# Score products of two heads, or of two maps, recorded alternately and issued as one set

## Chip, cores and metric

The kernel runs on one core of a Trainium2 chip. The metric is device microseconds of one execution, from the first to the last instruction and what lies around them; smaller is better. Engines are named as in the profile: PE is TensorE's matmul, PEld its weight load, DVE VectorE, ACT ScalarE, POOL GpSimd, SP the engine that issues the DMAs.

## What is computed

The reference runs two transformer blocks of two layers each on 256 tokens of width 1024, in fp32. A layer of block 1 is a gated feed-forward layer, a mixer and a second feed-forward layer; a layer of block 2 is a mixer and a feed-forward layer. The mixer of block 1 has four kinds of attention with four heads each, whose outputs are joined and projected:

- na: each token sees a window of a 4 x 64 grid, with a bias that is learned; head width 64
- diff: two maps per head, each from query and key of width 32, `a = softmax(s1) - lam * softmax(s2)`, with `s = q k^T / sqrt(32)`
- gqa: four query heads, two key and value heads, width 64, plain softmax
- dil: a mixture of three dilated windows, width 64

```python
        s = jnp.einsum('ibhqd,ibhkd->ibhqk', qblk, k12).astype(jnp.float32) * scale
        p = jax.nn.softmax(s, axis=-1)
        a = p[0] - lam * p[1]
        return jnp.einsum('bhqk,bhkd->bhqd', a.astype(vt.dtype), vt)
```

The mixer of block 2 has fox (4 causal heads with a decay), moba (4 causal heads of width 64 with a relative bias) and mla (8 causal heads of width 96). In both blocks a head is: scores q k^T, softmax, product with v.

## The kernel before, in words

**A plan, then the issue.** Nothing is issued while the kernel's functions run. Each call records an instruction in `Plan.add` (line 100), with what it depends on, the tiles that it touches and a cost in ns (`cost`, line 148; a matmul of rounded fp32, F32R, costs n / 2.4 + 2.5 ns for n columns). `order` (line 179) then places all instructions of the program by a list schedule with priorities from a backward pass (`priorities` and `backward`, lines 306 and 324), and `issue` (line 301) emits them in that order, so each engine's stream is fixed before the chip runs. All are emitted at one line, so all rows of the profile say L304, and groups are told by their tiles. Matmuls of one head can so be parted by any other PE work.

**Precision.** Operands are split into a high and a low F32R part. `mm3` (line 607) makes a product of three matmuls, high x high, high x low, low x high, added up in PSUM. moba, fox and mla use plain fp32 instead, with one matmul each.

**Mixers.** `mixer1` (line 1041) and `mixer2` (line 1398) run the input projection in chunks of 512 columns (`inproj`, line 986), prepare q and k (norm, rotation, transposes to the tiles qkT) and start attention heads as soon as their inputs are recorded. A head is a generator: `diff_job` (line 928), `job` (line 885, for dil, gqa and na) or `causal_job` (line 1339, for mla, fox and moba). `pump` (line 728) takes every started generator one step further after each half chunk and starts one more job of a list, with at most six in flight. `outproj` (line 1012) follows, and the last heads run beside it.

**One head.** `job` takes one PSUM bank (`aps`, line 749, tile att), writes the scores of 2 x 128 queries against 256 keys into it (two `mm3`, six matmuls of 256 columns), and has DVE and ACT make the softmax. Then come four transposes (tile tp, `turn_p`, line 919), a copy to SBUF (tile pt), the product with v into another bank (att<-V,pt), and a division. `diff_job` makes two maps so, i = 0 and i = 1, twelve matmuls of 256 columns in two banks. `causal_job` makes two matmuls, of 128 and of 256 columns.

**Rows of the array.** A matmul uses the rows of the array that correspond to the partitions of its operands. For head h, `mixer1` takes partitions 64 * (h % 2) on of dil and na, 64 * (h // 2) on of gqa; moba takes 64 * (h % 2) on. These products use 64 rows, of the upper or of the lower half. diff uses 32 rows, those from here on:

```python
            b = 64 * (h % 2) + 32 * i
            for t in range(2):
                tok = slice(t * P, t * P + P)
                self.mm3(sc[:, t * S:t * S + S], qT[0][b:b + 32, tok], qT[1][b:b + 32, tok], kT[0][b:b + 32], kT[1][b:b + 32], True, True)
```

mla and fox use 96 and 66 rows. In the profile's rows, 64*128 and 32*128 ahead of the shape are the rows and columns of the array. PSUM banks for att come from the four banks of tag y during the input projection, and in turn from tags mm and y during the output projection.

Of the kernel before, what the change touches and what calls it, by code (L numbers as in the profile page):

```python
# [72 lines left out]
class Plan:  # L73
# [26 lines left out]
    def add(self, eng, method, args, kw):  # L100
# [42 lines left out]
        self.ops.append([eng, method, args, kw, sorted(deps), sorted(touch), cost, after, table])  # L143

# [307 lines left out]
class Net:  # L452
# [432 lines left out]
    def job(self, kind, l, h, q, k, vh, col, bias=None):  # L885

        nc, V = self.nc, self.nc.vector
        sc = self.aps()
        for t in range(2):
            self.mm3(sc[:, t * S:t * S + S], q[0][:, t * P:t * P + P], q[1][:, t * P:t * P + P], *k, True, True)  # L890
        p = self.m(512, "p")
        nm = self.sm.tile([P, 2], F32, tag="nm", name="nm")
        if bias is not None:
            e = self.m(512, "e")
            for t in range(2):
                V.tensor_tensor_reduce(e[:, t * S:t * S + S], sc[:, t * S:t * S + S], bias[:, t], -0.125, 3e38,
                                       ALU.add, ALU.min, nm[:, t:t + 1])
            for t in range(2):
                nc.scalar.activation(p[:, t * S:t * S + S], e[:, t * S:t * S + S], AF.Exp, bias=nm[:, t:t + 1], scale=-1.0)
        else:  # L900
            V.tensor_reduce(nm, sc.rearrange("p (t k) -> p t k", t=2), axis=AX.X, op=ALU.max, negate=True)
            V.tensor_scalar(nm, nm, 0.125, None, op0=ALU.mult)
            for t in range(2):
                nc.scalar.activation(p[:, t * S:t * S + S], sc[:, t * S:t * S + S], AF.Exp, bias=nm[:, t:t + 1], scale=0.125)
        yield
        pt = self.turn_p(p)
        yield
        pv = self.aps()
        for t in range(2):
            for kt in range(2):  # L910
                nc.tensor.matmul(pv[:, t * 65:t * 65 + 65], lhsT=pt[:, (t * 2 + kt) * P:(t * 2 + kt + 1) * P],
                                 rhs=self.V[:, kt, vh, :], start=kt == 0, stop=kt == 1)
# [4 lines left out]
        self.done[kind] = self.done.get(kind, 0) + 1  # L917
# [10 lines left out]
    def diff_job(self, kind, l, h, qT, kT, vh, col):  # L928
# [3 lines left out]
        for i in range(2):  # L932
            sc = self.aps()
            b = 64 * (h % 2) + 32 * i
            for t in range(2):
# [105 lines left out]
    def mixer1(self, l, ydone, mid, pre):  # L1041
# [43 lines left out]
        for kind, vf, v0, col in (("dil", "v1", 4, 768), ("gqa", "vgqa", 8, 512), ("na", "vna", 10, 0)):  # L1085
            if kind == "na":
                self.jobs.append((lambda: True, lz(lambda: self.na_bias_mask(bias))))
            for h in range(4):
                def mk(kind=kind, v0=v0, col=col, h=h):
                    T = qkT[kind]  # L1090
                    b, base = (h % 2, 64 * (h // 2)) if kind == "gqa" else (h // 2, 64 * (h % 2))
                    kb = 0 if kind == "gqa" else h // 2
                    vh = v0 + (h // 2 if kind == "gqa" else h)
                    bb = None if kind == "gqa" else self.lnm if kind == "dil" else bias[h]
                    return self.job(kind, l, h, [a[base:base + 64, b] for a in T[0]], [a[base:base + 64, kb] for a in T[1]], vh, col + 64 * h, bb)
# [572 lines left out]
```

## Time and profile before

| what | us |
|---|---|
| median of three runs (lowest, highest) | 1653.28 (1652.83, 1656.73) |
| the profiled execution | 1654.43 |
| its span, first to last instruction | 1652.7 |
| PE busy | 1627.0 |
| DVE busy | 1085.4 |
| ACT busy | 842.3 |
| POOL busy | 167.9 |

The profiled execution lies 1.7 us above its span and 1.15 above the median. Mean granted clock of TensorE is 0.989 of full speed. The timeline gives the start and duration of instructions, and merges neighbours of one engine that have the same tiles into one row with their number (xN); its duration goes from the first start to the last end. As matmuls are pipelined, a row overlaps the next one: what PE spends on it is the distance to the next row's start.

### The profile page before, as it was taken

How to read it: one execution, taken by the hardware profiler on the slowest of the kernel's cores; microseconds unless marked ns; L12 is line 12 of the kernel's file. 1: busy time of each engine (PE TensorE's matmuls, PEld its weight loads, DVE VectorE, ACT ScalarE, POOL GpSimd, SP SyncE). 2: the span in 40 equal slices, each digit the busy share in tenths (PEclk: the TensorE clock that was granted, in tenths of full speed). 3: DMA queues.
4: the chain of work that ended last, by engine and by line, in shares of the span. 5: the costliest groups of instructions: out<-in, count | busy, mean ns of one | idle time of the engine just before them, and what ended most of it. 6: DMA issues, size and time to landing. Idle time of an engine off the chain costs nothing.

```text
span 1652.7 us, 21333 instructions
## 1 busy us (share of the span) xinstructions
PE 1627.0 (98%) x7912; PEld 1347.2 (82%) x7912; DVE 1085.4 (66%) x1956; ACT 842.3 (51%) x1384; POOL 167.9 (10%) x205
## 2 busy tenths in 40 slices
PE   9989999999999999999999999999999999999998
PEld 7868877888888888877788888888888888888886
DVE  6557778577777877777757645656755476585553
ACT  6544456554434444455554444576644358664442
POOL 0000056000000000035400000120000012000000
PEclk9989999999999999998899999999999999999999
DMA  8687762257776777763328645451645445245451
GB/s 305 221 268 283 264 220 103 77 224 301 267 293 245 300 293 267 289 220 120 110 75 311 245 178 195 171 180 53 242 180 202 153 162 207 101 171 202 176 203 51
DMA packets 81884, 335.78 MB, mean 203 GB/s; under 512 B 17136, under 2 KB 19700, under 8 KB 50676
## 3 DMA queue, kind: packets, MB, share of 16 engines
q1 hardware_dynamic: 81780, 334.42, 55.7%
q8 instruction: 62, 1.02, 0.2%
q14 instruction: 42, 0.34, 0.1%
HBM read 333.29 MB, written 2.84 MB: 203 GB/s over the span
## 4 chain that ended last, share of the span: by engine, by line
PE 92%; DVE 3%; POOL 2%; DMA 1%; issue 1%; ACT 1%; SPq 0%; POOLq 0%; DVEq 0%; ACTq 0%
PE mm L304 54%; PE y L304 27%; PE att L304 6%; PE tp L304 6%; DMA raw<-in_gu 1%; DVE wlo L304 1%; POOL rs L304 1%; POOL qk L304 0%; POOL rot L304 0%; DVE o L304 0%; DVE qk L304 0%; DVE ms L304 0%; DVE xl L304 0%; SPq L304 0%; DMA t5t<-in_t_table 0%
## 5 line engine op out<-in xcount | busy, mean ns | idle before, releaser
L304 DVE TENSOR_TENSOR wlo<-raw,whi 128x1024 fp32r<-128x1024 f32 (+2 forms) x516 | 607.2, 1211 | 263.2 <-ACT whi L304 261.4
L304 ACT CAST whi<-raw 128x1024 fp32r<-128x1024 f32 (+2 forms) x516 | 513.4, 1038 | 316.3 <-PE mm L304 132.1
L304 PE MATMUL mm<-whi,xh 128*128 128x512 f32 (+2 forms) x1376 | 547.0, 398 | 2.5 <-ACT whi L304 1.5
L304 PE MATMUL mm<-wlo,xh 128*128 128x512 f32 (+2 forms) x1376 | 537.3, 391 | 0.7 <-DVE wlo L304 0.7
L304 PE MATMUL mm<-whi,xl 128*128 128x512 f32 (+2 forms) x1376 | 534.8, 390 | 1.6 <-DVE xl L304 1.6
L304 PEld LDWEIGHTS mm<-whi,xl 128*128 128x128 f32 x1376 | 259.9, 189 | 55.7 <-DVE xl L304 2.9
L304 PEld LDWEIGHTS mm<-whi,xh 128*128 128x128 f32 x1376 | 259.9, 189 | 55.3 <-ACT whi L304 2.3
L304 PEld LDWEIGHTS mm<-wlo,xh 128*128 128x128 f32 x1376 | 260.4, 189 | 50.5 <-DVE wlo L304 1.6
L304 PE MATMUL y<-whi,hth 128*128 128x512 f32 x528 | 206.9, 393 | 0.0
L304 PE MATMUL y<-wlo,hth 128*128 128x512 f32 x528 | 206.6, 391 | 0.0
L304 PE MATMUL y<-whi,htl 128*128 128x512 f32 x528 | 206.5, 391 | 0.0
L304 POOL TENSOR_TENSOR rs<-rs,mhalf 128x1 f32<-128x1 f32 x28 | 27.2, 972 | 1267.2 <-DVE rs L304 1267.2
L304 ACT ACTIVATE sil<-mm 128x256 f32<-128x256 f32 x110 | 42.2, 384 | 210.4 <-PE mm L304 209.7
L304 DVE CUSTOM_DVE_ANT_0 ada<-ada,act 128x512 f32<-128x512 f32 x192 | 128.5, 688 | 17.3 <-DMA ada<-in_ada 16.9
L304 PEld LDWEIGHTS y<-wlo,hth 128*128 128x128 f32 x528 | 99.7, 189 | 21.6 <-issue 1.3
L304 PEld LDWEIGHTS y<-whi,htl 128*128 128x128 f32 x528 | 99.7, 189 | 20.9
L304 PEld LDWEIGHTS y<-whi,hth 128*128 128x128 f32 x528 | 99.5, 189 | 20.7 <-ACT whi L304 0.2
L304 DVE TENSOR_TENSOR hch<-mm,sil 128x256 f32<-128x256 f32 x110 | 46.3, 421 | 78.9 <-ACT sil L304 78.5
L304 PE MATMUL att<-qkT 64*128 64x256 f32 (+6 forms) x368 | 65.6, 321 | 1.8 <-DVE qkT L304 1.5
L304 POOL TENSOR_TENSOR rs<-ms,mhalf 128x2 f32<-128x2 f32 (+3 forms) x34 | 50.9, 1499 | 135.8 <-DVE ms L304 134.2
L304 PEld LDWEIGHTS att<-V,pt 128*128 128x128 f32 x448 | 59.5, 196 | 6.3 <-ACT pt L304 2.3
L304 PE MATMUL att<-V,pt 128*128 128x65 f32 (+1 forms) x448 | 60.0, 273 | 1.9 <-ACT pt L304 1.9
(158 smaller groups left out, 1388.1 us busy)
## 6 DMA issues: line engine op xcount, KB each, us to landing
raw<-in_gu SPq DMA_DIRECT2D x127, 1024.0 KB, 4.9
raw<-in_dn SPq DMA_DIRECT2D x66, 1024.0 KB, 4.9
ada<-in_ada SPq DMA_DIRECT2D x192, 256.0 KB, 5.3
raw<-in_in SPq DMA_DIRECT2D x32, 1024.0 KB, 4.8
raw<-in_out SPq DMA_DIRECT2D x16, 1024.0 KB, 4.8
row<-moddram SPq DMA_DIRECT2D x12, 512.0 KB, 6.8
raw<-in_in2a SPq DMA_DIRECT2D x4, 840.0 KB, 4.2
raw<-in_gu SPq DMA_DIRECT2D x6, 512.0 KB, 6.1
```

Of the source, the lines that this page charges most:

```text
L304: getattr(getattr(self.nc, eng), method)(*args, **kw)
```

## The change

Three things are done. In `diff_job` the matmuls of the two maps are recorded alternately (i = 0, i = 1, i = 0, ...), which makes six pairs with 32 rows each. `job` and `causal_job` take a list of heads and record the matmuls of two heads alternately: heads 0 and 1 and heads 2 and 3 of dil, na and moba, heads 0 and 2 and heads 1 and 3 of gqa, so that the two lie in different halves of the partitions. Each of the two has its own PSUM bank. And a new method `fuse` replaces the recorded matmuls by one entry of the plan, with the sum of their costs, all their dependencies and tiles; `issue` emits its matmuls one after the other. mla and fox keep one head a job, but their two matmuls become such an entry too. The rest of a head (softmax, transposes, product with v) is recorded per head as before, for both heads of a job within one step of the generator; there are half as many jobs of dil, gqa, na and moba.

```diff
@@ -141,6 +141,23 @@
+    def fuse(self, i0):
+        run = self.ops[i0:]
+        del self.ops[i0:]
+        eng = run[0][0]
+        assert all(o[0] == eng for o in run)
+        deps = sorted({d for o in run for d in o[4] if d < i0})
+        touch = sorted({t for o in run for t in o[5]})
+        self.ops.append([eng, "fused", [o[1:4] for o in run], {}, deps, touch, sum(o[6] for o in run), 0, None])
+        for a in self.write.values():
+            a[a > i0] = i0
+        for k, r in self.read.items():
+            if r and r[-1][0] > i0:
+                self.read[k] = [(min(j, i0), idx) for j, idx in r]
+        self.last_mm = i0
...
@@ -301,7 +318,8 @@
     def issue(self):
         for i in self.order(self.priorities())[0]:
             eng, method, args, kw = self.ops[i][:4]
-            getattr(getattr(self.nc, eng), method)(*args, **kw)
+            for m, a, k in args if method == "fused" else [(method, args, kw)]:
+                getattr(getattr(self.nc, eng), m)(*a, **k)
...
-    def job(self, kind, l, h, q, k, vh, col, bias=None):
+    def job(self, kind, heads):
...
-        sc = self.aps()
+        sc = [self.aps() for _ in heads]
+        i0 = len(nc.ops)
         for t in range(2):
-            self.mm3(sc[:, t * S:t * S + S], q[0][:, t * P:t * P + P], q[1][:, t * P:t * P + P], *k, True, True)
-        p = self.m(512, "p")
-        nm = self.sm.tile([P, 2], F32, tag="nm", name="nm")
-        if bias is not None:
-            e = self.m(512, "e")
+            for a, b, start, stop in ((0, 0, True, False), (0, 1, False, False), (1, 0, False, True)):
+                for s, (q, k, _, _, _) in zip(sc, heads):
+                    nc.tensor.matmul(s[:, t * S:t * S + S], lhsT=q[a][:, t * P:t * P + P], rhs=k[b], start=start, stop=stop)
+        nc.fuse(i0)
+        ps = []
+        for s, (_, _, _, _, bias) in zip(sc, heads):
+            p = self.m(512, "p")
...
+            ps.append(p)
+        yield
+        pts = [self.turn_p(p) for p in ps]
+        yield
+        for pt, (_, _, vh, col, _) in zip(pts, heads):
+            pv = self.aps()
...
+            self.weigh(pv, col)
+        self.done[kind] = self.done.get(kind, 0) + 2
...
+    def weigh(self, pv, col):
...
@@ -930,13 +961,17 @@
         for i in range(2):
-            sc = self.aps()
-            b = 64 * (h % 2) + 32 * i
-            for t in range(2):
-                tok = slice(t * P, t * P + P)
-                self.mm3(sc[:, t * S:t * S + S], qT[0][b:b + 32, tok], qT[1][b:b + 32, tok], kT[0][b:b + 32], kT[1][b:b + 32], True, True)
-            ps.append(sc)
-            V.tensor_reduce(nm[:, 2 * i:2 * i + 2], sc.rearrange("p (t k) -> p t k", t=2), axis=AX.X, op=ALU.max, negate=True)
+            ps.append(self.aps())
+        i0 = len(nc.ops)
+        for t in range(2):
+            tok = slice(t * P, t * P + P)
+            for a, c, start, stop in ((0, 0, True, False), (0, 1, False, False), (1, 0, False, True)):
+                for i in range(2):
+                    b = 64 * (h % 2) + 32 * i
+                    nc.tensor.matmul(ps[i][:, t * S:t * S + S], lhsT=qT[a][b:b + 32, tok], rhs=kT[c][b:b + 32], start=start, stop=stop)
+        nc.fuse(i0)
+        for i in range(2):
+            V.tensor_reduce(nm[:, 2 * i:2 * i + 2], ps[i].rearrange("p (t k) -> p t k", t=2), axis=AX.X, op=ALU.max, negate=True)
...
@@ -1085,14 +1120,17 @@
-            for h in range(4):
-                def mk(kind=kind, v0=v0, col=col, h=h):
+            for hs in ((0, 2), (1, 3)) if kind == "gqa" else ((0, 1), (2, 3)):
+                def mk(kind=kind, v0=v0, col=col, hs=hs):
...
+                    heads = []
+                    for h in hs:
+                        b, base = (h % 2, 64 * (h // 2)) if kind == "gqa" else (h // 2, 64 * (h % 2))
+                        kb = 0 if kind == "gqa" else h // 2
+                        vh = v0 + (h // 2 if kind == "gqa" else h)
+                        bb = None if kind == "gqa" else self.lnm if kind == "dil" else bias[h]
+                        heads.append(([a[base:base + 64, b] for a in T[0]], [a[base:base + 64, kb] for a in T[1]], vh, col + 64 * h, bb))
+                    return self.job(kind, heads)
                 self.jobs.append((has(kind, vf), lz(mk)))
...
-    def causal_job(self, kind, q, k, vh, col, bias, scale):
+    def causal_job(self, kind, heads, bias, scale):
...
-        sc = self.aps()
+        sc = [self.aps() for _ in heads]
         span = (slice(0, P), slice(P, 384))
+        i0 = len(nc.ops)
-            nc.tensor.matmul(sc[:, span[t]], lhsT=q[:, t * P:t * P + P], rhs=k[:, 0:P * (t + 1)], start=True, stop=True)
...
+            for s, (q, k, _, _) in zip(sc, heads):
+                nc.tensor.matmul(s[:, span[t]], lhsT=q[:, t * P:t * P + P], rhs=k[:, 0:P * (t + 1)], start=True, stop=True)
+        nc.fuse(i0)
+        ps = []
+        for i, s in enumerate(sc):
...
+            ps.append(p)
+        yield
+        pts = []
+        for p in ps:
...
+            pts.append(pt)
+        yield
+        for pt, (_, _, vh, col) in zip(pts, heads):
+            pv = self.aps()
...
+            self.weigh(pv, col)
+        self.done[kind] = self.done.get(kind, 0) + len(heads)
...
@@ -1432,21 +1478,24 @@
         def heads(kind, v0, g):
-            for h in range(4):
-                def mk(h=h):
...
+            for hs in [(h,) for h in range(4)] if kind == "fox" else [(0, 1), (2, 3)]:
+                def mk(hs=hs):
+                    A, bias = [], []
+                    for h in hs:
...
+                        A.append((q, k, v0 + h, g * 256 + 64 * h))
+                    return self.causal_job(kind, A, bias, 0.125)
                 J.append((has(kind, "v"), lz(mk)))
...
-                return self.causal_job("mla", st["q"][h // 2][0:96, h % 2], st["k"][h // 2][0:96, h % 2], 8 + h, 512 + 64 * h,
-                                       (self.causal[:, P:S], self.causal), 96 ** -0.5)
+                return self.causal_job("mla", [(st["q"][h // 2][0:96, h % 2], st["k"][h // 2][0:96, h % 2], 8 + h, 512 + 64 * h)],
+                                       [(self.causal[:, P:S], self.causal)], 96 ** -0.5)
```

## Rows read from the trace of the kernel before

**Rows 1.** The page: PE's share of the span, and the chain by engine.

```profile
PE 1627.0 (98%) x7912; PEld 1347.2 (82%) x7912; DVE 1085.4 (66%) x1956; ACT 842.3 (51%) x1384; POOL 167.9 (10%) x205
...
PE 92%; DVE 3%; POOL 2%; DMA 1%; issue 1%; ACT 1%; SPq 0%; POOLq 0%; DVEq 0%; ACTq 0%
```

**Rows 2.** Busy time in four stretches: start:end, length, engines, PEclk, DMA share, GB/s.

```profile
245.00:280.00 35.00, 34.19 (x195) 27.10 (x193) 34.38 (x90) 23.90 (x62) 22.77 (x27) 1.00 0.27 91
293.00:323.00 30.00, 30.00 (x206) 25.73 (x206) 16.44 (x47) 16.15 (x33) 3.06 (x3) 1.00 0.29 103
760.00:797.00 37.00, 36.03 (x188) 28.24 (x187) 31.30 (x81) 23.16 (x61) 24.97 (x26) 0.91 0.24 86
...
1128.00:1138.00 10.00, 10.00 (x74) 7.99 (x71) 7.45 (x32) 9.12 (x23) 0.19 (x1) 1.00 0.17 72
```

**Rows 3.** PE by line and form: count, busy us, mean ns, idle us before.

```profile
L304 PE MATMUL att<-qkT 64*128 64x256 f32 x160 | 30.0, 319 | 1.5 <-DVE qkT L304 1.5
...
L304 PE MATMUL att<-qkT 32*128 32x256 f32 x96 | 12.9, 318 | 0.3 <-ACT pd L304 0.3
...
L304 PE MATMUL att<-qkT 64*128 64x128 f32 x16 | 3.0, 320 | 0.0
```

**Rows 4.** PE timeline around a run of six: start us, duration us, instruction.

```profile
760.57 0.39 PE L304 MATMUL mm<-whi,xl 128*128 128x512 f32 x1
760.79 0.39 PE L304 MATMUL mm<-whi,xh 128*128 128x512 f32 x1
761.11 0.97 PE L304 MATMUL att<-qkT 32*128 32x256 f32 x6
762.01 0.49 PE L304 MATMUL mm<-wlo,xh 128*128 128x512 f32 x1
762.43 0.97 PE L304 MATMUL att<-qkT 32*128 32x256 f32 x6
```

**Rows 5.** PE timeline: one product, two in different rows, two serial, a mixed run.

```profile
312.19 0.38 PE L304 MATMUL att<-qkT 64*128 64x256 f32 x1
...
312.87 0.38 PE L304 MATMUL att<-qkT 64*128 64x256 f32 x2
...
321.76 0.50 PE L304 MATMUL att<-qkT 64*128 64x256 f32 x2
...
755.45 1.66 PE L304 MATMUL att<-qkT 32*128 32x256 f32 x24
```

**Rows 6.** PE timeline: first and last runs of gqa/na, dil, diff; three of moba.

```profile
242.76 0.58 PE L304 MATMUL att<-qkT 32*128 32x256 f32 x4
...
271.68 0.38 PE L304 MATMUL att<-qkT 64*128 64x256 f32 x1
...
293.52 0.97 PE L304 MATMUL att<-qkT 64*128 64x256 f32 x6
...
767.60 0.58 PE L304 MATMUL att<-qkT 32*128 32x256 f32 x1
...
803.32 1.43 PE L304 MATMUL att<-qkT 64*128 64x256 f32 x5
...
843.38 0.97 PE L304 MATMUL att<-qkT 64*128 64x256 f32 x6
...
1130.65 0.49 PE L304 MATMUL att<-qkT 64*128 64x128 f32 x2
...
1133.06 0.70 PE L304 MATMUL att<-qkT 64*128 64x256 f32 x2
...
1136.10 1.03 PE L304 MATMUL att<-qkT 64*128 64x128 f32 x8
...
1433.40 0.93 PE L304 MATMUL att<-qkT 64*128 64x128 f32 x8
```

**Rows 7.** A PE wait in its timeline, and the stretch behind it by windows.

```profile
799.87 1.97 PE L304 MATMUL att<-V,pt 128*128 128x65 f32 x8 [1.85 <-ACT pt L304]
...
799.70:810.00 10.30, 10.13 (x32) 7.85 (x33) 3.54 (x14) 3.58 (x8) 3.05 (x3) 0.50 0.13 56
```

More of the change, by code (lines that the diff above doesn't have):

```diff
@@ new lines, in job @@
+            for a, b, start, stop in ((0, 0, True, False), (0, 1, False, False), (1, 0, False, True)):
[5 more added lines that the diff above has]
+            p = self.m(512, "p")
+            nm = self.sm.tile([P, 2], F32, tag="nm", name="nm")
+            if bias is not None:
+                e = self.m(512, "e")
+                for t in range(2):
+                    V.tensor_tensor_reduce(e[:, t * S:t * S + S], s[:, t * S:t * S + S], bias[:, t], -0.125, 3e38,
+                                           ALU.add, ALU.min, nm[:, t:t + 1])
+                for t in range(2):
+                    nc.scalar.activation(p[:, t * S:t * S + S], e[:, t * S:t * S + S], AF.Exp, bias=nm[:, t:t + 1], scale=-1.0)
+            else:
+                V.tensor_reduce(nm, s.rearrange("p (t k) -> p t k", t=2), axis=AX.X, op=ALU.max, negate=True)
+                V.tensor_scalar(nm, nm, 0.125, None, op0=ALU.mult)
+                for t in range(2):
+                    nc.scalar.activation(p[:, t * S:t * S + S], s[:, t * S:t * S + S], AF.Exp, bias=nm[:, t:t + 1], scale=0.125)
+            ps.append(p)
@@ new lines, in job @@
+        yield
[3 more added lines that the diff above has]
+            pv = self.aps()
+            for t in range(2):
+                for kt in range(2):
+                    nc.tensor.matmul(pv[:, t * 65:t * 65 + 65], lhsT=pt[:, (t * 2 + kt) * P:(t * 2 + kt + 1) * P],
+                                     rhs=self.V[:, kt, vh, :], start=kt == 0, stop=kt == 1)
+            self.weigh(pv, col)
+        self.done[kind] = self.done.get(kind, 0) + 2
@@ new lines, in causal_job @@
+            for s, (q, k, _, _) in zip(sc, heads):
[3 more added lines that the diff above has]
+        for i, s in enumerate(sc):
+            p = self.m(384, "p")
+            e = self.m(384, "e")
+            nm = self.sm.tile([P, 2], F32, tag="nm", name="nm")
+            for t in range(2):
+                V.tensor_tensor_reduce(e[:, span[t]], s[:, span[t]], bias[i][t], -scale, 3e38, ALU.add, ALU.min, nm[:, t:t + 1])
+            for t in range(2):
+                nc.scalar.activation(p[:, span[t]], e[:, span[t]], AF.Exp, bias=nm[:, t:t + 1], scale=-1.0)
+            ps.append(p)
@@ new lines, in causal_job @@
+        yield
+        pts = []
+        for p in ps:
+            tp = self.tp()
+            for b in range(3):
+                nc.tensor.transpose(tp[:, b * P:b * P + P], p[:, b * P:b * P + P], self.ident)
+            pt = self.m(384, "pt")
+            self.copy(pt, tp[:, 0:384])
+            pts.append(pt)
+        yield
+        for pt, (_, _, vh, col) in zip(pts, heads):
+            pv = self.aps()
+            for t in range(2):
+                for kt in range(t + 1):
+                    nc.tensor.matmul(pv[:, t * 65:t * 65 + 65], lhsT=pt[:, (t + kt) * P:(t + kt + 1) * P],
+                                     rhs=self.V[:, kt, vh, :], start=kt == 0, stop=kt == t)
+            self.weigh(pv, col)
```

60 lines of the change are left out of this document (8 added, 52 removed).

## The prediction

> **What bounds the kernel now.** I read the page's share of each engine first, then the chain that ended last, then busy times by stage, and last the PE timeline of the four attention stretches. TensorE is busy 98% of the span and holds 92% of the chain [rows 1]: time taken from PE's stream comes off the end, unless another engine is as late. The windows say where one is [rows 2]. While the heads diff and dil run beside the input projection (245 to 280 us, first layer of block 1), DVE is busy 34.4 of 35 us, as full as PE; in the second layer (760 to 797) 31.3 of 37. While gqa and na run (293 to 323) PE is full, DVE is at 16.4 of 30 us and ACT at 16.2; in block 2 around moba (1128 to 1138) PE is full and DVE has a quarter free, though ACT has only a tenth.
>
> The products in question are the 64-row and 32-row forms, 176 and 96 instructions [rows 3]; mla and fox have others. In the timeline they stand in 54 runs between other PE work.
>
> **What a run costs.** Projection matmuls start 0.22 us apart. From the last one before a run of six to the run 0.32, from there to the next projection 0.90, and that one holds the array 0.42 before the following run, where half of the extra 0.20 is the next run's entry [rows 4]. So a run of six costs 0.10 + 0.90 + 0.10 = 1.10 us. A run of one lasts 0.38, one of six 0.97 [rows 4, 5]: each further product in the same rows adds (0.97 - 0.38) / 5 = 0.118. Hence a run costs 0.39 us for going in and out, plus 0.118 per product.
>
> Two products in different rows cost what one costs: at 312.87 a run of two lasts 0.38, like the single one at 312.19; at 321.76 two of one head last 0.50. A run of 24, in which the plan had happened to mix heads, lasts 1.66, (1.66 - 0.38) / 23 = 0.056 each [rows 5]. So overlap exists on this chip with these tiles, and part of it is already had.
>
> **The change, part by part.** Number and size of the instructions stay; the order, and what may stand between them, change. A set of 12 (six pairs) costs 0.39 + 6 x 0.118 = 1.10 us, what one head of six costs now.
>
> - gqa and na (first run at 293.52, last at 843.38, 21 runs, 96 products [rows 6]): now 21 x 0.39 + 96 x 0.118 = 19.5, less 0.2 for two pairs that already overlap. After: 8 sets x 1.10 = 8.8. Saved 10.5 us.
> - moba (8 runs, 32 products, plain fp32; rows show the second and the last [rows 6]): two of 128 columns last 0.49, two of 256 last 0.70, so a further one adds about 0.11 or 0.22. Entry and exit add about 0.12 to a run's duration. Per layer: four serial (0.49 + 0.44 + 0.12 = 1.05), two short (0.61), two long (0.82), and eight that already overlap (1.03 + 0.12): 3.6. After: two sets of four, each 0.49 - 0.11 + 0.22 + 0.12 = 0.72: 1.4. Saved 2.2 a layer, 4.3 for both, as the other eight last 0.93.
> - dil (271.68 to 803.32, 11 runs, 48 products [rows 6]): 11 x 0.39 + 48 x 0.118 = 9.95, less 0.35 of overlap in the first run of twelve; after 4 x 1.10. Saved 5.2.
> - diff (242.76 to 767.60, 14 runs, 96 products, 48 of them in three mixed runs at 0.056 [rows 5, 6]): 14 x 0.39 + 48 x 0.118 + 48 x 0.056 = 13.8; after 8 x 1.10 = 8.8, dearer than now for the mixed ones, as a pair uses two quarters of the rows where they used up to four. Saved 5.0.
>
> Together 25.0 us of PE time. gqa, na and moba (14.8) lie where PE alone is full; I take all of it. dil and diff (10.2, half in each layer) lie beside a full DVE. There a PE that is early waits for DVE, which splits the weights it needs. In the first layer I take nothing of the 5.1; in the second, where DVE has 15% free, two thirds, 3.4. Sum 18.2.
>
> mla and fox only lose the freedom to have other work between their two matmuls; the work is the same, and I take nothing for it, with the bounds of the next paragraph.
>
> What the edits add: a set waits for q and k of both heads and for two PSUM slots, and the projections and transposes behind it in PE's queue wait with it. No row shows such a set. Bounds: nothing, since diff jobs take two slots already; or the longest wait of attention on PE, 1.85 us [rows 7], once in each of the four mixers, 7.4. I take nothing, because DVE and ACT, who give the slots back, are half free in the long stretch [rows 2] and the first head's scores arrive as early as now (1.10 us for both against 1.10 for one). The second head's softmax starts earlier than now. DVE, ACT and DMA instructions stay as many; no DMA is moved, though the order of all queues is planned anew from the new recording. The plan books a set at its serial price, 12 x (256/2.4 + 2.5) ns = 1.31 us, and did not know the 0.39; it was too short for a head and is now too long for a pair, so PE will come early rather than late.
>
> Against the profiled execution (1654.43 us, 1.15 above the median of 1653.28): 1654.4 - 18.2 = 1636.2, or **1635** against the median.
>
> **A rule that speaks against it.** Rows 2 show DVE full in the diff and dil stretch and half free later. The Trainium skill, TensorEngine Tiling (Array Packing), section Performance Considerations, says that tiling speeds up TensorE but not the emptying of PSUM, which may become the bottleneck. By that rule all of the 10.2 us would be lost, and more if it held for gqa and na too; the rows bear it out for the first layer only.
>
> **The rivals.**
> 1. Everything counts: DVE's work in 245 to 280 is itself released by scores, so it starts earlier too. 25.0 us saved, 1628; if the wait of 1.85 us and the half-clock stretch behind it (799.7 to 810 at 0.50 [rows 7], which costs 10.3 / 2 = 5.15) also go, 1621. For it: PE holds the chain. Against: 34.4 of 35 us.
> 2. DVE's emptying of PSUM takes all of diff and dil: 14.8 saved, 1638.5. This is the rule's case, worked out from rows 2 and the sums above.
> 3. PE runs dry and its clock falls (slower). At 797.6 to 799.9 PE waited 1.85 us for an ACT copy, and then had 1.2 instead of 2.4 GHz for 10.3 us [rows 7]: 7.0 us for one such event. With 25 us less PE work in stretches where POOL and DVE set the pace, and a set that waits for two heads, more of them can come. Two new ones give 1635 + 14 = 1649, no change that can be told; the point of no gain lies at 18.2 / 7.0 = 2.6; four, one in each mixer, give 1663. Against it: one mixer in two of block 1, and none of block 2, has such an event now.
> 4. The pairs don't overlap, because consecutive products of a pair wait for each other's accumulation: a set then costs 0.39 + 12 x 0.118 = 1.81. gqa and na save 4.8, moba 3.0, dil and diff 1.7, of which a third: 8.4 in all, 1645. The run of 24 speaks against it.
>
> **How the numbers follow.** About 0.3%, 5 us, is what a measurement of this kernel can tell from no change: 1648.3 to 1658.3. Chances: forecast 0.50, rival 1 0.18, rival 2 0.10, rival 4 0.03, so faster 0.81; two new events, no change, 0.11; four, slower, 0.08. The range reaches down to rival 1 with the recovered clock (1621, less a microsecond) and up to the two events (1649, and one more): 1620 to 1650. It leaves out the slower case and the edges, under 2 in 10.
>
> **What would show it.** In the profile after: 32-row and 64-row products again 96 and 176, in about 24 runs instead of 54; runs of twelve that last about 0.97 instead of 0.97 for six; PE busy down by some 18 to 25 us; DVE and ACT with the same number of instructions; the stretch of gqa and na about 5 us shorter in each layer. Runs of twelve near 1.7 us would show rival 4. New PE waits for DVE or ACT in 240 to 280 with the front of dil at the same time as now would show rival 2, and new stretches at clock 0.50 rival 3. A longer time with none of these would mean that the plan reordered something I did not look at, and my sum would be wrong.

## The result, and the profile after

The changed kernel takes **1627.27 us** (median of 4 runs, 1626.13 to 1627.82); the kernel before, measured beside it, 1653.05 (1651.83 to 1656.73). The ratio is 0.9839 [0.9823, 0.9854]: 25.8 us or 1.6% faster. The forecast was 1635 within 1620 to 1650, so sign and range were right, and the forecast gain was 7.7 us too small; rival 1, in which everything counts, said 1628. The profiled execution is the fastest of the four (1626.13, span 1624.3); between the two profiled spans lie 28.4 us.

The page, to be laid against the first line of [rows 1], and PE by line and form, against [rows 3] (the new code makes every line L322):

```profile
PE 1597.1 (98%) x7912; PEld 1328.5 (82%) x7912; DVE 1080.4 (67%) x1956; ACT 838.7 (52%) x1384; POOL 158.8 (10%) x205
```

```profile
L322 PE MATMUL att<-qkT 64*128 64x256 f32 x160 | 15.1, 321 | 2.6 <-ACT qkT L322 1.2 <-DVE qkT L322 1.1 <-DVE ov L322 0.3
...
L322 PE MATMUL att<-qkT 32*128 32x256 f32 x96 | 7.8, 293 | 0.0
...
L322 PE MATMUL att<-qkT 64*128 64x128 f32 x16 | 2.0, 323 | 0.0
```

Every engine has its old number of instructions. The busy time of the three forms fell from 45.9 to 24.9 us, and PE's from 1627.0 to 1597.1 (29.9, of which a part is the clock, below). PE's wait ahead of these products grew from 1.5 us [rows 3] to 2.6, of which 2.3 are for dil's q and k.

The PE timeline (start, duration, instruction), to be laid against [rows 4, 5]:

```profile
289.14 0.39 PE L322 MATMUL mm<-whi,xh 128*128 128x512 f32 x1
289.46 0.98 PE L322 MATMUL att<-qkT 64*128 64x256 f32 x12
290.37 0.50 PE L322 MATMUL mm<-wlo,xh 128*128 128x512 f32 x1
...
310.28 1.69 PE L322 MATMUL att<-qkT 64*128 64x256 f32 x24
...
1102.71 0.93 PE L322 MATMUL att<-qkT 64*128 64x128 f32 x8
1103.56 0.55 PE L322 MATMUL tp<-ident,p 128*128 128x128 f32 x3
```

Twelve products now last 0.98 where six lasted 0.97: 0.91 to the next instruction, and 0.10 + 0.10 of entry and exit, 1.11 where the forecast has 1.10. The 54 runs have become 24 sets, some of them back to back, so that 21 runs are left.

Busy time by stage (start:end, length, the engines, PEclk, DMA share, GB/s), against [rows 2]:

```profile
245.00:280.00 35.00, 32.49 (x210) 26.96 (x208) 34.06 (x98) 26.46 (x69) 21.28 (x26) 0.95 0.26 91
289.00:314.00 25.00, 24.59 (x196) 21.57 (x195) 17.83 (x45) 16.29 (x33) 3.03 (x3) 1.00 0.37 127
728.00:850.00 122.00, 117.18 (x731) 97.69 (x730) 93.13 (x218) 74.91 (x153) 44.15 (x47) 1.00 0.38 132
272.00:275.40 3.40, 3.35 (x24) 3.04 (x25) 3.40 (x14) 1.38 (x3) 2.69 (x4) 0.50 0.77 260
1100.00:1110.00 10.00, 9.56 (x74) 7.59 (x72) 8.34 (x40) 10.00 (x26) 0.00 (x0) 1.00 0.25 99
```

In the first layer's diff and dil stretch PE now has gaps (32.5 of 35), while DVE is as full as before (34.1 of 35): [rows 2] had both full. Around moba ACT is full, 10.00 of 10. The second layer's mixer, which had clock 0.50 in three places, has 1.00 throughout.

**Where the time went.** The eight transposes of the first half of `hn` stand ahead of each mixer and again behind it; in the PE timeline after they are these, for the two mixers of block 1 (333.48 - 202.35 = 131.1, and 127.6):

```profile
202.35 1.03 PE L322 MATMUL tp<-ident,hn 128*128 128x128 f32 x8
...
333.48 1.04 PE L322 MATMUL tp<-ident,hn 128*128 128x128 f32 x8
...
708.04 1.03 PE L322 MATMUL tp<-ident,hn 128*128 128x128 f32 x8
...
835.63 1.04 PE L322 MATMUL tp<-ident,hn 128*128 128x128 f32 x8
```

Before, the same rows start at 203.25, 340.16, 714.70 and 862.32. In block 2 a mixer is taken from such a row of eight to a row of four transposes of `hn` behind it: before 1049.64 to 1160.90 and 1346.67 to 1458.13, after 1022.97 to 1133.24 and 1318.98 to 1429.53. Half-clock time is read from the granted clock; "clock out" is the length less half of it, an estimate of what the mixer would take at full clock.

| mixer | before, us | of it at half clock | after, us | at half clock | shorter | clock out |
|---|---|---|---|---|---|---|
| block 1, first layer | 136.9 | 3.4 | 131.1 | 6.8 | 5.8 | 7.5 |
| block 1, second layer | 147.6 | 20.5 | 127.6 | 0 | 20.0 | 9.8 |
| block 2, first | 111.3 | 0 | 110.3 | 0 | 1.0 | 1.0 |
| block 2, second | 111.5 | 0 | 110.6 | 0 | 0.9 | 0.9 |

That is 27.7 of the 28.4 us between the two profiles: 19.2 of work and 8.5 of clock.

The cost of all runs with entry and exit, both layers, summed from the traces (the neighbours are taken at their full-clock price, so what a run and its neighbours lose at half clock is in it):

| kind | before, us | after, us | saved | forecast |
|---|---|---|---|---|
| gqa and na | 18.6 | 8.1 | 10.5 | 10.5 |
| dil | 11.7 | 6.2 | 5.5 | 5.2 |
| diff | 15.9 | 8.9 | 7.0 | 5.0 |
| moba | 6.96 | 4.04 | 2.9 | 4.3 |
| sum | | | 25.9 | 25.0 |

### The profile page after: what moved, and what is told of

Same layout as the page of the kernel before. It is cut to its first block, busy times and chain, and to the rows that moved or that the text cites. A ratio compares the mean times of both kernels' runs of the same rounds, so it can differ in the third digit from the quotient of the medians.

```text
span 1624.3 us, 21308 instructions
## 1 busy us (share of the span) xinstructions
PE 1597.1 (98%) x7912; PEld 1328.5 (82%) x7912; DVE 1080.4 (67%) x1956; ACT 838.7 (52%) x1384; POOL 158.8 (10%) x205
## 4 chain that ended last, share of the span: by engine, by line
PE 79%; DVE 3%; ACT 2%; POOL 1%; issue 1%; DVEq 0%; POOLq 0%; ACTq 0%
PE mm L322 46%; PE y L322 24%; PE tp L322 5%; PE att L322 4%; POOL rs L322 1%; DVE wlo L322 1%; DVE nm L322 0%; POOL rot L322 0%; ACT p L322 0%; DVE pd L322 0%; DVE o L322 0%; ACT pd L322 0%; ACT whi L322 0%; DVE ss L322 0%; DVE qkT L322 0%
## 5 line engine op out<-in xcount | busy, mean ns | idle before, releaser
L322 DVE TENSOR_TENSOR wlo<-raw,whi 128x1024 fp32r<-128x1024 f32 (+2 forms) x516 | 605.5, 1206 | 252.7 <-ACT whi L322 252.0
L322 ACT CAST whi<-raw 128x1024 fp32r<-128x1024 f32 (+2 forms) x516 | 512.6, 1036 | 308.6 <-PE mm L322 127.9
L322 PE MATMUL mm<-whi,xh 128*128 128x512 f32 (+2 forms) x1376 | 544.6, 396 | 1.8 <-ACT xh L322 0.9
L322 PE MATMUL mm<-wlo,xh 128*128 128x512 f32 (+2 forms) x1376 | 536.0, 390 | 0.3 <-DVE wlo L322 0.2
L322 PE MATMUL mm<-whi,xl 128*128 128x512 f32 (+2 forms) x1376 | 533.8, 389 | 0.5 <-DVE xl L322 0.5
L322 PEld LDWEIGHTS mm<-whi,xl 128*128 128x128 f32 x1376 | 259.4, 189 | 53.1 <-DVE xl L322 1.2
L322 PEld LDWEIGHTS mm<-whi,xh 128*128 128x128 f32 x1376 | 259.3, 188 | 52.6 <-ACT xh L322 1.9
L322 PEld LDWEIGHTS mm<-wlo,xh 128*128 128x128 f32 x1376 | 259.6, 189 | 49.6 <-DVE wlo L322 1.1
L322 PE MATMUL y<-whi,hth 128*128 128x512 f32 x528 | 206.7, 393 | 0.0
L322 PE MATMUL y<-wlo,hth 128*128 128x512 f32 x528 | 206.5, 391 | 0.0
L322 PE MATMUL y<-whi,htl 128*128 128x512 f32 x528 | 206.2, 391 | 0.0
L322 ACT ACTIVATE sil<-mm 128x256 f32<-128x256 f32 x110 | 42.3, 384 | 207.7 <-PE mm L322 207.0
L322 POOL TENSOR_TENSOR rs<-rs,mhalf 128x1 f32<-128x1 f32 x28 | 26.2, 934 | 1235.2 <-DVE rs L322 1235.2
L322 DVE CUSTOM_DVE_ANT_0 ada<-ada,act 128x512 f32<-128x512 f32 x192 | 128.6, 690 | 20.5 <-DMA ada<-in_ada 20.2
L322 PEld LDWEIGHTS y<-wlo,hth 128*128 128x128 f32 x528 | 99.6, 189 | 21.4 <-issue 1.3
L322 PEld LDWEIGHTS y<-whi,htl 128*128 128x128 f32 x528 | 99.6, 189 | 20.8
L322 PEld LDWEIGHTS y<-whi,hth 128*128 128x128 f32 x528 | 99.5, 189 | 20.8 <-ACT whi L322 0.2
L322 DVE TENSOR_TENSOR hch<-mm,sil 128x256 f32<-128x256 f32 x110 | 46.4, 422 | 77.7 <-ACT sil L322 77.3
L322 POOL TENSOR_TENSOR rs<-ms,mhalf 128x2 f32<-128x2 f32 (+3 forms) x34 | 47.2, 1390 | 133.0 <-DVE ms L322 131.7
L322 PEld LDWEIGHTS att<-V,pt 128*128 128x128 f32 x448 | 56.3, 191 | 4.6 <-issue 1.3
L322 PE MATMUL att<-V,pt 128*128 128x65 f32 (+1 forms) x448 | 57.5, 269 | 1.2 <-DVE o L322 0.9
L322 DVE TENSOR_TENSOR htl<-tp,hth 128x512 fp32r<-128x512 f32 x66 | 45.0, 689 | 11.8 <-ACT hth L322 11.5
```

Of the source, the lines that this page charges most:

```text
L322: getattr(getattr(self.nc, eng), m)(*a, **k)
```

## The experiments

The change does three things at once: products that had stood apart now stand together (fused), two heads alternate, and the two lie in different rows. My theory was the forecast's: each run costs 0.39 us of going in and out, and products in different rows cost half. Rivals: alternation does it all, or standing together does it all, or the clock does it. All ratios are to the kernel before on the same chip, in brackets the 95% interval. Every variant is planned anew, so some of each difference can be order alone; the kernel of experiment 9, in which only the order changes, lies 1.4 us from the changed one.

**1. Together, but not alternating.** Inside a set, the loop over the heads (or maps) goes outermost.

```diff
-        for t in range(2):
-            for a, b, start, stop in ((0, 0, True, False), (0, 1, False, False), (1, 0, False, True)):
-                for s, (q, k, _, _, _) in zip(sc, heads):
+        for s, (q, k, _, _, _) in zip(sc, heads):
+            for t in range(2):
+                for a, b, start, stop in ((0, 0, True, False), (0, 1, False, False), (1, 0, False, True)):
```

> The changed kernel with its sets, but inside a set the first head's products stand ahead of the second's (and map 0 ahead of map 1), so that neighbours use the same rows. Theory (overlap): the saving is array time that two products share; a set of twelve then costs 0.39 + 12 x 0.118 = 1.81 us instead of 1.10, 20 sets lose 14.2, four sets of moba some 0.66 each, so about 17 us of PE work come back: 1644 us, or up to 1654 if the clock falls again in the second layer. Rival (grouping): fewer runs and the new plan make the gain, the order inside a set nothing: 1627 to 1630.

Measured: 1629.23, 0.9864 [0.9849, 0.9878], nearly the whole gain. The timeline of this kernel:

```profile
293.64 1.32 PE L322 MATMUL att<-qkT 64*128 64x256 f32 x12
294.89 0.50 PE L322 MATMUL mm<-wlo,xh 128*128 128x512 f32 x1
...
315.11 2.03 PE L322 MATMUL att<-qkT 64*128 64x256 f32 x24
...
1110.74 0.93 PE L322 MATMUL att<-qkT 64*128 64x128 f32 x8
```

The expectation that such a set costs its serial price missed. Six products of one head followed by six of the other take 1.25 to the next instruction; alternating ones took 0.91. All runs together cost 32.9 us against 27.2, and of these 5.7 us 2 (by the medians) to 4 (by the ratios) show in the time; the two intervals overlap. So alternation is worth 0.34 us to a set of twelve by itself, half of that where two sets stand back to back (2.03 against 1.69 for 24) and nothing to a set of moba (0.93 both ways), and it is not where the gain comes from.

**2. The same partition rows.** Partners in the same half, still alternating: for gqa heads (0, 1), (2, 3), for the others (0, 2), (1, 3). diff's maps stay in different quarters.

```diff
-            for hs in ((0, 2), (1, 3)) if kind == "gqa" else ((0, 1), (2, 3)):
+            for hs in ((0, 1), (2, 3)) if kind == "gqa" else ((0, 2), (1, 3)):
...
-            for hs in [(h,) for h in range(4)] if kind == "fox" else [(0, 1), (2, 3)]:
+            for hs in [(h,) for h in range(4)] if kind == "fox" else [(0, 2), (1, 3)]:
```

> The changed kernel with other partners: heads 0 and 2, 1 and 3 of dil, na and moba, heads 0 and 1, 2 and 3 of gqa, which lie in the same half of the partitions. Sets, their order and the plan's prices stay; diff keeps its pairs. Theory (overlap needs different rows; TensorE starts products of other rows that stand a few places behind): inside such a set nothing overlaps, a set of twelve costs 0.39 + 12 x 0.118 = 1.81 us, one of moba 0.66 more than now; 12 and 4 of them give 8.5 + 2.6 = 11 us, less about 2 where two sets are neighbours and lie in different halves: 1634 to 1639. Rival (grouping alone, as the small loss of the serial sets might be read): within 3 us of the changed kernel, 1625 to 1630.

Measured: 1634.47, 0.9888 [0.9872, 0.9904]. Its timeline:

```profile
292.38 1.68 PE L322 MATMUL att<-qkT 64*128 64x256 f32 x12
293.99 0.50 PE L322 MATMUL mm<-wlo,xh 128*128 128x512 f32 x1
...
314.57 2.75 PE L322 MATMUL att<-qkT 64*128 64x256 f32 x24
...
1109.60 1.57 PE L322 MATMUL att<-qkT 64*128 64x128 f32 x8
```

Here twelve take 1.61 to the next, with 0.10 + 0.10 beside it 1.81: rival 4's price. All runs cost 10.3 us more than in the changed kernel, and the time is 7 us longer, with intervals that don't overlap. Laid beside experiment 1, this shows that different rows are what makes products of two heads overlap, and that the heads need not alternate for it.

**3. Together one by one.** Each head (for diff, each map) is a set of its own of six products.

```diff
-            for hs in ((0, 2), (1, 3)) if kind == "gqa" else ((0, 1), (2, 3)):
+            for hs in ((0,), (1,), (2,), (3,)):
```

> The changed kernel with one head (or one map) a set: products of a head can't be parted, and no two heads are mixed. Theory (overlap and entries): 40 sets of six cost 1.10 each, as 20 sets of twelve pairs do now, so 22 us of PE work come back, and the chance overlaps of the kernel before are gone: 1648 to 1656 us. Rival (grouping): keeping a head's products together is most of it: 1630 to 1638.

Measured: 1645.66, 0.9963 [0.9948, 0.9978]. 39 runs are left, which cost 47.5 us. A quarter of the gain comes from a head that no projection parts any more; the rest needs two heads in one set. The steps so far, by the ratios: 0.4% for one head a set, 1.1% for two in the same rows (diff's two maps still in different ones), 1.4% for two in different rows one after the other, 1.6% for alternating ones. Clock and work are both in these steps: the mean granted clock of the runs is 0.991 with one head a set and 0.993 in the three others. In the timeline of this kernel a set of six costs what it cost before:

```profile
810.05 0.97 PE L322 MATMUL att<-qkT 64*128 64x256 f32 x6
810.95 0.38 PE L322 MATMUL mm<-whi,xh 128*128 128x256 f32 x1
```

**4. Alternating, but free.** The three `nc.fuse(i0)` are removed.

```diff
-        nc.fuse(i0)
```

> The changed kernel without the fusing: products of two heads are recorded alternately, and the plan may put other PE work between them. Theory: they become ready together and have neighbouring priorities, so most pairs stay adjacent and overlap; each time a run is cut costs 0.39 us. 1628 to 1634 us. Rival (the set as one entry is what matters): the plan scatters them as it did before, about 54 runs, 1640 to 1650.

Measured: 1635.47, 0.9904 [0.9887, 0.992]; 43 runs, 43.5 us. Recorded alternately, the products are still parted by the plan, and a pair left alone pays the whole entry. Timeline:

```profile
288.44 0.39 PE L322 MATMUL att<-qkT 64*128 64x256 f32 x2
...
305.88 0.38 PE L322 MATMUL att<-qkT 64*128 64x256 f32 x1
```

**5 and 6. diff alone, and all but diff.** The kernel before with only the new `diff_job`, `fuse` and `issue`; and the changed kernel with the old `diff_job`, whose edit is shown.

```diff
-        i0 = len(nc.ops)
-        for t in range(2):
...
-        nc.fuse(i0)
-        for i in range(2):
...
+            sc = self.aps()
+            b = 64 * (h % 2) + 32 * i
+            for t in range(2):
+                tok = slice(t * P, t * P + P)
+                self.mm3(sc[:, t * S:t * S + S], qT[0][b:b + 32, tok], qT[1][b:b + 32, tok], kT[0][b:b + 32], kT[1][b:b + 32], True, True)
```

> The kernel before with the change in diff alone. Runs of diff cost 15.9 us before and 8.9 after in the two traces, 3.0 saved in the first layer and 3.9 in the second. Theory (DVE holds the first layer's stretch, and the clock of the second layer falls behind long stretches of 32-row runs): nothing in the first layer, 3.9 in the second, and the half-clock stretch at 765 to 772 (3.4 us lost) goes: about 1646 us. Rival (the clock's recovery does not hang on diff): 1649 to 1651. Rival (PE holds the end in both layers): 1643.

> The changed kernel with diff as before. Runs of dil, gqa, na and moba cost 37.3 us before and 18.3 after. Theory: gqa and na give their 10.5, moba 2, dil about half of 5.5, and the stretch at half clock behind the diff heads of the second layer stays (3.4 lost): 1635 to 1638 us. Rival (the clock's recovery comes from dil, gqa and na): 1628 to 1632.

Measured: diff alone 1648.44, 0.9975 [0.996, 0.9991]; all but diff 1636.12, 0.9894 [0.9868, 0.992]. By the ratios these are 4 and 17.5 us. With diff alone the first layer's mixer gained nothing (137.8 against 136.9), the second's 3.6 with the clock out. The sum, 21.6, is 5 short of the 26.6 that the changed kernel has by its ratio, about what the three intervals together leave uncertain. In the kernel without the diff change, a stretch at half clock lies behind diff's second-layer runs, as it did before, while PE is busy without a gap; the kernel with it alone has full clock there, and its half-clock stretches (748.2 to 751.7 and 782.4 to 792.6) stand behind waits of PE for q and k. Busy time by stage, first without, then with diff's change; the third fence is the kernel before:

```profile
758.00:764.80 6.80, 6.80 (x22) 4.78 (x22) 5.33 (x14) 3.02 (x10) 1.52 (x2) 0.50 0.00 0
```

```profile
757.00:775.00 18.00, 17.89 (x114) 14.25 (x113) 16.18 (x42) 16.38 (x47) 8.44 (x14) 1.00 0.19 60
```

```profile
765.60:772.40 6.80, 6.80 (x24) 5.06 (x23) 4.70 (x13) 3.11 (x11) 2.52 (x2) 0.50 0.00 0
```

**7. moba alone.** The kernel before with only block 2's jobs as changed.

```diff
-            nc.tensor.matmul(sc[:, span[t]], lhsT=q[:, t * P:t * P + P], rhs=k[:, 0:P * (t + 1)], start=True, stop=True)
...
+            for s, (q, k, _, _) in zip(sc, heads):
+                nc.tensor.matmul(s[:, span[t]], lhsT=q[:, t * P:t * P + P], rhs=k[:, 0:P * (t + 1)], start=True, stop=True)
+        nc.fuse(i0)
```

> The kernel before with block 2's mixer as changed. Its runs cost 7.0 us before and 4.0 after; block 2's two mixers are 1.1 and 0.9 us shorter in the changed kernel's trace. Theory: 2.0 us less, 1651; block 1 is planned alone and its half-clock stretches stay. Rival (one plan for the whole program: a change in block 2 moves block 1 too): a difference of more than 4 us either way.

Measured: 1652.01, 0.9994 [0.9978, 1.0009]: nothing that can be told. The block 2 mixers are 0.8 shorter and 0.7 longer.

**8 and 9. Four maps in a set, and the plan's price.** In the first, diff's set holds the four maps of two heads, 24 products in all four quarters of the rows (for this the plan's test for a free PSUM slot no longer counts an entry's own tiles against it). In the second the plan books a set at what it costs. The third kernel has both (with 1.08 / n in place of 0.54, for n banks in a set). First the edit of the price, then that of the four maps:

```diff
-        self.ops.append([eng, "fused", [o[1:4] for o in run], {}, deps, touch, sum(o[6] for o in run), 0, None])
+        cost = sum(o[6] for o in run)
+        if len({o[2][0].tensor.name for o in run}) > 1:
+            cost = 390 + 0.54 * cost
+        self.ops.append([eng, "fused", [o[1:4] for o in run], {}, deps, touch, cost, 0, None])
```

```diff
-                    if free[k] <= c or place[t] > head[k] and max(held[k][head[k]:place[t]]) + c >= self.slots[k]:
+                    p0 = min(place[u] for u in ops[i][5] if u not in live and self.slot_of[u] == k)
+                    if free[k] <= c or p0 > head[k] and max(held[k][head[k]:p0]) + c >= self.slots[k]:
...
-                for i in range(2):
-                    b = 64 * (h % 2) + 32 * i
...
+                for s, (h, qT, kT, _) in zip(ps, heads):
+                    for i in range(2):
+                        b = 64 * (h % 2) + 32 * i
...
-        for h in range(4):
...
+        for hs in ((0, 1), (2, 3)):
```

> The changed kernel with diff in sets of four maps (two heads), 24 products that use all four quarters of the rows in turn. If four in different quarters cost what one costs (0.118), a set of 24 costs 1.10 us, as one of 12 does, and 4.4 us of PE work go. Theory (DVE holds the first layer's stretch and PE has waits there): half or less of that is seen, 1624 to 1627. Rival (PE holds the end everywhere): 1622 to 1623. Slower, if four banks at once hold up other heads: over 1628.

> The changed kernel with the plan's price of a paired set put at what rows show: 390 ns plus 0.54 of the serial sum, 1.10 us instead of 1.31 for twelve. The work is the same. Theory (the plan's error on a set is small against its others): within 2 us of 1627. Rival (PE comes early by 0.2 us a set and waits, 24 sets): up to 5 us less, 1622.

> Both together: diff in sets of four maps, and the plan's price of a set as the rows show it (390 ns plus 1.08 / n of the serial sum for n banks). Each alone was within 1 us of the changed kernel. Theory (the stretch of dil and diff is held by DVE, ACT and POOL; the plan's price moves only the order): 1622 to 1627. Rival (the price lets the plan use the shorter sets): 1618 to 1621.

Measured: four maps 1626.47, 0.9841 [0.9827, 0.9856]; the true price 1625.87, 0.9829 [0.9805, 0.9853]; both 1626.65, 0.9847 [0.983, 0.9864]. None is told from the changed kernel's 0.9839. Yet the four maps do take what a pair takes, as the timeline shows, and PE has 4.4 us less to do:

```profile
249.08 0.98 PE L323 MATMUL att<-qkT 32*128 32x256 f32 x24
249.99 0.50 PE L323 MATMUL mm<-whi,xh 128*128 128x512 f32 x1
```

PE work taken from diff is thus worth nothing here any more. The clock hides a part of this: the runs with four maps have a mean granted clock of 0.996, the changed kernel's 0.993. With the clock out the two mixers of block 1 take 127.7 and 129.3 us, where the changed kernel has 127.7 and 127.6. What PE saved, it waited for elsewhere: from 720 to 850 us its waits come to 7.7 us with four maps and to 4.7 without, and the largest that is new is for diff's maps to be combined:

```profile
PE tp L323 <- DVE pd L323: 1.6, 2, 1.2
```

What holds the end of the first layer's stretch?

**10 and 11. Without the rotation.** So that q and k are ready earlier, the rotation of q and k of dil and gqa (four POOL instructions each time) is left out, so these two kinds compute something else. The second kernel has the four maps in a set too.

```diff
-                 2: ("dil", [(4, G[:, 64:128]), (4, G[:, 128:192])], 64, (16, 16, 8)),
+                 2: ("dil", [(4, G[:, 64:128]), (4, G[:, 128:192])], 64, None),
```

> The changed kernel without the rotation of q and k of dil and gqa (POOL's four operations for each), so that their qkT is ready earlier. It computes something else there. The first layer's mixer of block 1 is 117.3 us long in the changed kernel, with 2.3 us of PE waits for dil's qkT and a stretch of 3.4 us at half clock behind them; with the clock counted out 113.9. Theory (what dil's inputs wait for, not PE, sets the diff and dil stretch of the first layer): the waits and the stretch go, 113 us, and 1621 to 1625 in all. Rival (DVE's own work holds it): the mixer stays within 1 us of 114 with the clock counted out.

> The same without that rotation, and diff in sets of four maps, which takes 4.4 us of PE work off, half of it in each layer of block 1. Theory (once dil's inputs are there, PE holds the end of the diff stretch too): 1.5 to 2.2 us a layer shorter than the kernel without rotation and with pairs, 3 to 4.4 in all. Rival (DVE holds it in any case): within 1 us of it.

Measured: 1623.34, 0.9828 [0.9803, 0.9854], and 1620.01, 0.9804 [0.9771, 0.9837]. Without the rotation dil's two waits and the half-clock stretch behind them are gone, and the first layer's mixer is 3.4 shorter; but with the clock out it is 127.7, as in the changed kernel and as the rival expected of it, since other waits came. In the second layer the mixer is 2.0 shorter with the clock out. PE's waits from 215 to 335 us (who, for what, us in total, times, the longest; the three largest), first in the changed kernel, then without the rotation:

```profile
PE tp L322 <- POOL qk L322: 2.4, 1, 2.4
PE att L322 <- ACT qkT L322: 1.2, 1, 1.2
PE att L322 <- DVE qkT L322: 1.1, 1, 1.1
```

```profile
PE tp L322 <- POOL qk L322: 2.8, 1, 2.8
PE tp L322 <- ACT p L322: 1.2, 2, 0.8
PE tp L322 <- DVE pd L322: 1.0, 2, 0.6
```

The wait of 2.8 ends at 238.26, ahead of diff's heads: it is for diff's own q and k, whose rotation was left in. Leaving POOL's work out also shortened DVE's: the same 1956 instructions took 1074.8 us instead of 1080.4, so the experiment does not tell POOL's rotation from DVE's load.

And now the four maps pay: 3.3 us, where they paid nothing with the rotation in. The two intervals overlap, and 1.6 to 2.0 of the 3.3 go with a higher granted clock (0.9953 against 0.9940 over four runs each; an estimate by the slope worked out below), so the times alone don't carry it; but the mixers of the profiles say the same with the clock out: 2.4 less in the first layer, 1.0 in the second. What the other engines prepare for dil and gqa therefore very likely covers a part of what PE saves in diff.

**Which step it is for dil.** The trace of the changed kernel answers this. The last four transposes of dil's q and k end at 264.35. DVE, busy 13.74 of 14 us from 262 to 276, splits q only at 269.66 and k at 271.58, each time behind a split of weights, and ACT's cast of k waits for the first of the two. The two waits of PE end 0.05 us behind that cast and behind the second split (DVE, then ACT, with the idle time before it in brackets):

```profile
268.11 1.62 DVE L322 TENSOR_TENSOR wlo<-raw,whi 128x1024 fp32r<-128x1024 f32 x1
269.66 0.41 DVE L322 TENSOR_TENSOR qkT<-tp,qkT 128x256 fp32r<-128x256 f32 x1
...
270.45 1.22 DVE L322 TENSOR_TENSOR wlo<-raw,whi 128x1024 fp32r<-128x1024 f32 x1
271.58 0.41 DVE L322 TENSOR_TENSOR qkT<-tp,qkT 128x256 fp32r<-128x256 f32 x1
```

```profile
270.10 0.37 ACT L322 CAST qkT<-tp 128x256 fp32r<-128x256 f32 x1 [3.88 <-DVE qkT L322]
```

## Why the prediction was right, and where it was off

**The price of a run held.** 0.39 for going in and out and 0.118 a product gave 1.10 for a set of twelve; the sets cost 0.91 + 0.20. gqa and na came out at the 10.5 us forecast, though both sides of it were 0.7 too high (19.3 forecast for 18.6 before, 8.8 for 8.1 after). All runs came out at 25.9 for 25.0, and that is partly luck: diff was 2.0 too low, moba 1.4 too high. diff's 7.0 for 5.0 is this: about 1.7 us of its cost before was time lost at half clock by its products and their neighbours, which my unit prices of full-clock rows didn't hold.

**moba was mis-sized,** 4.3 for a measured 2.9. I read "two sets of four" off the count of rows, but each of these plain fp32 matmuls stands as two records: a set of four matmuls has eight ([rows 6] has one such run already, 1433.40, 0.93). A set costs 0.86 and its entry, not 0.72. And where PE gave 2.9, the two mixers became only 1.9 shorter. ACT is full there, which would explain it, but no run tests that; alone the change in block 2 was worth nothing that can be told.

**"Nothing in the first layer, two thirds in the second"** was close as a sum and somewhat low in both. With the clock out the layers gained 7.5 and 9.8, where gqa, na, dil and diff had 5.25 and 8.65 by the forecast; with moba's 1.9 for 4.3 the errors offset each other, which is why 18.2 and 19.2 of work lie so close. In the first layer 9.7 us of runs were saved and 7.5 came, so of the 4.3 in dil and diff about half, if gqa and na count in full. By the timeline that half is dil's: the products of dil that waited start 69.7 us behind the mixer's start (272.05 - 202.35), before 69.3 (272.56 - 203.25), so diff's 3.0 brought nothing there, as with diff alone, and the whole gain lies behind them. The reason given, a PE that is early and waits for a full DVE, holds, but not for the weights: PE waited 0.2 us for DVE's split of these in the whole span and 2.3 for dil's q and k, whose split stands behind that of the weights in DVE's queue. New waits at a front of dil that comes no earlier were the sign set for rival 2, and in the first half of that mixer its outcome was right; its reason, the emptying of PSUM, was not.

The Trainium skill, TensorEngine Tiling (Array Packing), section Performance Considerations, says that the emptying of PSUM may become the bottleneck when TensorE gets faster. As a rule of the whole it does not fit this case: rival 2's 1638.5 was 11 us too long, and the waits shown for the changed kernel are for q and k being prepared, not for scores being emptied. Only with the rotation out and four maps in a set is PE's longest wait from 245 to 335 us one for a PSUM bank, which ACT's exponentials of diff were still reading:

```profile
PE att L323 <- ACT pd L323: 1.3, 1, 1.3
```

**What was missed is the clock.** The forecast of 18.2 was of work, and 19.2 came. The other 8.5 us of the profiles are 17.1 us less at half clock: 20.5 gone in the second layer, 3.4 new in the first. I had put a recovered clock into rival 1 alone, and only for the stretch behind the wait of 1.85 us [rows 7]. That wait and its stretch did go, but so did the two others of the second layer, at 752.0 and 765.6:

```profile
752.00:755.40 3.40, 3.40 (x9) 2.22 (x7) 2.42 (x5) 0.67 (x2) 2.92 (x3) 0.50 0.57 241
755.40:765.60 10.20, 10.20 (x66) 7.83 (x65) 7.52 (x17) 7.04 (x20) 3.81 (x7) 1.00 0.01 2
728.60:862.30 133.70, 127.63 (x694) 104.17 (x693) 89.95 (x211) 71.86 (x145) 53.66 (x51) 0.92 0.31 103
```

(Busy time by stage in the kernel before; the second row is what PE did ahead of 765.6, and the last is nearly the whole second-layer mixer, mean clock 0.92, where after has 1.00.) One profile is one execution. The mean granted clock is 0.9895 over the 41 runs of the kernel before that stand beside the experiments, and 0.993 in each of the four after. Among the runs of the unchanged kernel the time follows it: on one chip 1657.0 us at 0.987 and 1645.29 at 0.994, about 1.6 us for 0.001; a straight line through all 41 gives 1.3. By these slopes some 5 of the 25.8 us are clock and 20 are work, an estimate.

**Rival 3 happened once, in small.** PE waited 1.16 and 1.14 us for dil's q and k, and the clock was at 0.50 from 272.0 to 275.4, at a cost of about 4 us in the first layer. It is a wait ahead of a set, which I had costed at nothing with a bound of 7.4:

```profile
270.53 0.38 PE L322 MATMUL att<-qkT 64*128 64x256 f32 x2 [1.16 <-ACT qkT L322]
272.05 2.71 PE L322 MATMUL att<-qkT 64*128 64x256 f32 x22 [1.14 <-DVE qkT L322]
274.69 0.80 PE L322 MATMUL mm<-whi,xh 128*128 128x512 f32 x1
```

(PE timeline after, in brackets the idle time before and what ended it.) But it isn't the wait for a second head: `prep` makes q, or k, of all four dil heads in one instruction for 128 tokens, and the kernel with one head a set waited 1.31 and 1.55 us in the same places. PE came early, as rival 3 says: the last projection ahead of dil starts 66.6 us behind the mixer's start, before 68.1, and k was ready at 69.6, before 69.3. That such stretches would be outnumbered by others that vanish was not foreseen. The argument against rival 3 also misread the rows (the wait of 1.85 us began at 798.0, not 797.6): it found such an event in one mixer of block 1, but both had one ahead of diff's heads as well, a wait for diff's q and k with half clock behind it (240.0 to 243.4 and 752.0 to 755.4), in the kernel before:

```profile
239.06 0.66 PE L304 MATMUL tp<-ident,qk 128*128 128x128 f32 x4 [1.86 <-POOL qk L304]
...
750.75 0.66 PE L304 MATMUL tp<-ident,qk 128*128 128x128 f32 x4 [2.16 <-POOL qk L304]
```

**Rival 4** had the right price for the wrong case. 1.81 holds for two heads in the same rows, 1.81 measured; for the changed kernel its reason, pairs that wait for each other, is false.

**Open:** which step, beside DVE's split for dil, holds the rest of the first layer's stretch; and whether runs of six products cause the half-clock stretch behind diff. In the five profiled kernels whose later diff products stand in runs of six or fewer (behind one run of 24) it is there in the second layer, and in three of them in the first as well; in the nine with sets of twelve or more it is in neither. But this is one profile of each, and nothing else was held fixed.

## What to carry to other kernels

Products that use only a half or a quarter of the array's rows paid here for going in and out of that shape, 0.39 us a visit, more than three products of work. By the steps measured, gather them into few visits first, choose partners in different rows second, and think of their order within a visit last. When the bound engine gets faster, look in the same window at the engine that was nearly as full, and measure the clock apart from the work before crediting either. And once a stretch is held by others, as diff's was, further PE work saved there is worth nothing until they are relieved.

## What the runs showed of the hardware that was not expected

- TensorE overlapped products of different row halves even when all those of one head stood ahead of the other's: twelve in that serial order took 1.32 us, 0.98 when alternating, 1.68 when in the same rows; 24 in a row took 2.03, 1.69 and 2.75.
- Four quarters cost what two cost here: 24 products of 32 rows took 0.98 us, like twelve.
- The clock also fell where PE had been busy without a gap: in the kernel before 10.20 of 10.20 us ahead of 765.6 and 6.80 of 6.80 at half clock behind it, with 32-row products among projections.
- Most of the spread between runs of the kernel before goes with its mean granted clock, 1.3 to 1.6 us for 0.001.
- DVE's instructions lasted longer beside POOL's rotation: in the changed kernel two of 128x64 took 2.11 us while it ran (264.86 to 266.87), and 0.47 at 270.06:

```profile
264.84 2.11 DVE L322 SCALAR_TENSOR_TENSOR o<-ov,rs,og 128x64 f32<-128x64 f32 x2
...
270.06 0.47 DVE L322 SCALAR_TENSOR_TENSOR o<-ov,rs,og 128x64 f32<-128x64 f32 x2
```
